# Two products of four feature pairs, run ahead on half of the tokens, as the opening of a SwiGLU FFN

## The chip, the cores and the metric

The kernel runs on one core of a Trainium2 chip. The core has a matrix engine (TensorE, "PE" in the profile, with its weight loads as "PEld"), a vector engine (VectorE, "DVE"), a scalar engine (ScalarE, "ACT"), GpSimd ("POOL") and a queue engine that issues transfers (SyncE, "SP"). Matmuls write to PSUM, which has eight banks here; everything else lies in SBUF, and weights come from HBM by DMA. The metric is device microseconds of one execution; the median of several runs is taken.

## The reference

One layer on 512 tokens of width 1024, all in float32: an FFN, a token mixer (two attention branches, gates and an output projection), and a second FFN of its own weights.

```python
def _swiglu(x, w_gate, w_up, w_down):
    return (jax.nn.silu(x @ w_gate) * (x @ w_up)) @ w_down

f = _swiglu(_rmsnorm(x, ffn1_pre_g[l]), ffn1_w_gate[l], ffn1_w_up[l], ffn1_w_down[l])
x = x + 0.5 * _rmsnorm(f, ffn1_post_g[l])
```

`w_gate` and `w_up` are 1024 x 2816, `w_down` is 2816 x 1024. The change is in how both FFNs compute `x @ w_gate` and `x @ w_up`; the mixer between them is left as it is.

## The kernel before, in words

**Precision.** A float32 factor is split into a high part of reduced mantissa (type fp32r) and the rest, by one copy on ScalarE and one subtraction on VectorE (`split`, L109 to L112). A product then takes three matmuls: high x high, high x low, low x high (`mm3`, L189 to L192).

**Features and pieces.** The 2816 hidden features are 22 groups of 128 (`NF`); here a group is called a feature. For each there is a gate piece and an up piece of the weights, each 128 x 1024 (eight blocks of 128 x 128, one per 128 rows of the model width; 512 KB). The normalised tokens stand transposed in `hn_hi` and `hn_lo`, as model width by tokens, and are the moving operand. Gate and up of one feature are a "pair".

**Ordinary pairs.** `proj_into` (L194) multiplies one piece with the tokens: 8 blocks x 3 matmuls, over 512 tokens or 256. Before the change the first three features (`STD = 3`) are computed so. The first two of them go through `first_pairs` (L217): the last two token tiles are still being normalised and transposed when the FFN begins, so all four pieces are first multiplied with tokens 0 to 255 (24 matmuls of 256 columns each), with the transposes of token tiles 2 and 3 slipped in after two of them (`turns`), and then with tokens 256 to 511. The first piece runs in another order (`proj_first`), all products with the high parts of the tokens first. The third feature goes over the full width of 512 (`pair`, L208).

**Seven products.** The other 19 features are computed with seven block products in place of eight (`seven`, L344). A pair is seen as a 2 x 2 matrix of blocks: the two halves of the model width, by gate and up; the tokens as a 2 x 2 matrix too: halves of the model width by halves of the tokens. Products 1 and 2 are gate times tokens 0 to 255, one for each half of the model width. Products 3 to 7 use sums of weight blocks (named t1 to t4) and sums of token blocks (made once for each FFN by `combined`, L292, from `hn` and from `whole`, unsplit copies of tokens 256 to 511). Each product is 4 blocks x 3 matmuls of 256 columns, 84 for a pair. Products 1, 7, 6 and 4 gather in bank `q`, 5 and 3 in `p`, 2 in `r`; ScalarE and VectorE combine them in `g` and `up`. `use7` applies silu and multiplies.

**Weights.** `load_blocks` (L320) loads one pair's blocks: four transfers on SP's queue, and two on GpSimd's queue that add a second block to one already loaded (L329, L330), so that t1 and t3 arrive as sums. t2 and t4 are added on VectorE (`sums_of`, L335 and L336). `split_block` splits a block into a slot of the pool `w`, which has twelve slots of 128 x 1024. Whole pieces come through `fetch` and `convert` (L122): a load into one of two wide staging buffers (`raw`, L127), then a split of 1024 columns into two slots. A pair by seven products uses one staging buffer too.

**PSUM.** All banks come from one pool of eight (`bank`). A transposed token tile takes two banks (`turned`, L271). For tiles 2 and 3 they are kept until ScalarE has also copied them to `whole` (`kept`, `keep`, L286 to L289): eight copies, run after the last first-half product.

**Order.** From the start of an FFN's head to a mark after the head's first products, the instructions of TensorE, ScalarE and VectorE are pinned to program order among themselves (`ordered`); SP's are until the mixer starts. Elsewhere the framework's scheduler orders each engine's work by its own model, and may also put unpinned work between pinned instructions. Each engine then works strictly in the order it was given.

Of the kernel before, what the change touches and what calls it, by code (L numbers as in the profile page):

```python
# [20 lines left out]
P = 128  # L21
# [13 lines left out]
STD = 3  # L35
# [9 lines left out]
def block_kernel(ctx, tc, x, gains, weights, rpb_near, rpb_all, alibi0, alibi12, out):  # L45
# [71 lines left out]
    state = {"used": False, "next": 0, "take": 0, "stop": 2 * STD, "ahead": lambda: None}  # L117
# [99 lines left out]
    def first_pairs(use, turns, then=None, mid=None):  # L217
# [3 lines left out]
        for i in range(4):  # L221
            (proj_into if i else proj_first)(ps[i], w[i], 0, 256)
            if i in turns:
                late.popleft()()
                if next_norm:
                    next_norm.pop()()
        while kept:
            kept.popleft()()
        if then:
            then()  # L230
        fetch()
        fetch()
        if mid:
            mid(0)
        for i in range(4):
            proj_into(ps[i], w[i], 256, 512)
            if mid and i % 2:
                use(i // 2, *ps[i - 1:i + 1])
                mid(1 + i // 2)
        ordered[-1].append(mark())  # L240
        if not mid:
            use(0, *ps[:2])
            use(1, *ps[2:])


# [45 lines left out]
    def combined():  # L291
# [15 lines left out]
        v = {}  # L307
# [12 lines left out]
    def load_blocks(n):  # L320


        r = wp.tile([P, PIECE], F32, tag="raw", name="raw", bufs=2)
        w11, t1, t3 = unit(name="w11"), unit(name="t1"), unit(name="t3")
        nc.sync.dma_start(t1, weights[n + 1][:, :512])
        nc.sync.dma_start(t3, weights[n + 1][:, :512])
        nc.sync.dma_start(r, weights[n])
        nc.sync.dma_start(w11, weights[n + 1][:, 512:])
        nc.gpsimd.dma_start(t1, weights[n][:, :512], accum_op=ALU.add)  # L329
        nc.gpsimd.dma_start(t3, weights[n + 1][:, 512:], accum_op=ALU.add)  # L330
        return {1: r[:, :512], 2: r[:, 512:], 3: w11, 5: t1, 7: t3}

    def sums_of(raw):
        t2, t4 = unit(name="t2"), unit(name="t4")
        nc.vector.tensor_tensor(t2, raw[5], raw[3], op=ALU.add)  # L335
        nc.vector.tensor_tensor(t4, t2, raw[2], op=ALU.add)  # L336
        raw[6], raw[4] = t2, t4
# [6 lines left out]
    def seven(use, mv, n_pairs, n0, behind, far, lead, raws):  # L344
# [8 lines left out]
        def get(j):  # L353
            if j < n_pairs and j not in raws:
                raws[j] = load_blocks(n0 + 2 * j)
# [3 lines left out]
        def ready(j, i):  # L359
            if j < n_pairs:  # L360
# [4 lines left out]
                blocks[j, i] = split_block(raws[j].pop(i))  # L365
# [18 lines left out]
        for j in range(n_pairs + 1):  # L384
            now, was = j < n_pairs, j > 0
            get(j + 2)
            if now:
                q = product(j, 1, "q", True)
                g, u = res[j] = unit(name="g"), unit(name="up")
                nc.scalar.copy(g[:, :256], q)  # L390
# [10 lines left out]
            if now:  # L401
# [89 lines left out]
    def ffn(g, store, src):  # L491
# [6 lines left out]
        def times(j, a, b):  # L498

            k = feats.index(j)  # L500
            if k >= 2 * m or j < STD:
# [3 lines left out]
            to = lambda i, k: duos[i][k // 2][:, (k % 2) * 256:(k % 2) * 256 + 256]  # L505
            parts = [slice(i * 256, i * 256 + 256) for i in range(2)]
            for i, part in enumerate(parts):
                if duos[i][k // 2] is None:
                    duos[i][k // 2] = unit(name="h")
                nc.vector.tensor_tensor(to(i, k), a[:, part], b[:, part], op=ALU.mult)  # L510
            if k % 2 and hidden[k - 1] is not None:
                for i, part in enumerate(parts):
                    nc.gpsimd.tensor_copy(to(i, k - 1), hidden[k - 1][:, part])
                hidden[k - 1] = None
# [14 lines left out]
        def mid(i):  # L529
            if i == 0:  # L530
                for j in range(2):
# [1063 lines left out]
```

## Time and profile before

| What | Before |
|---|---|
| Timed runs, us | 1087.65, 1087.65, 1088.85 (median 1087.65) |
| Span of the profiled execution, us | 1086.5 |
| TensorE busy | 1076.5 us (99%), 6809 matmuls |
| VectorE / ScalarE / GpSimd busy | 827.5 / 653.1 / 185.6 us |
| Head of the first FFN, from its first product to the first of the seven products | 10.81 to 46.74 us |
| Head of the second FFN | 747.27 to 782.94 us |
| Loaded by SP's queue / by the adding loads of GpSimd's | 131.55 / 52.96 MB |

The profile is of one execution. Its rows name an engine, a line of the kernel (L192), the tiles written and read, shapes, and times in microseconds unless marked ns. In a timeline a row is: start, duration, engine, line, operation, tiles, shapes, count, and in brackets the idle time of the engine before it and what ended it. A timeline joins equal instructions that follow each other into one row. In a table by windows a row is: the window, its length, then for each engine the busy time and the instructions that touch it, the granted clock of TensorE as a share, the busy share of the DMA engines, and GB/s. Matmuls are pipelined, so their recorded durations overlap, and starts are what to compare.

### The profile page before, as it was taken

The page shows a single profiled execution, that of the slowest core. Times are in us where ns is not written, and L with a number is a line of the kernel's source. Part 1 is how long each engine was busy: PE and PEld are TensorE (multiplying, and loading weights), DVE is VectorE, ACT ScalarE, POOL GpSimd, SP SyncE. Part 2 cuts the span into 40 slices and gives each one's busy share as a digit, 9 for nine tenths or more (in the row PEclk, how much of TensorE's full clock was granted, in tenths as well). Part 3 has the DMA queues.
Part 4 walks back from the last instruction along what each step waited for, and adds up shares of the span by engine and source line. Part 5 has one row for each costly group of instructions (what it writes and reads, how often), then busy time and mean ns, then how long its engine had stood idle before and what let it go on. Part 6 is the DMA issues. An engine that isn't in the chain of part 4 may idle for free.

```text
span 1086.5 us, 18606 instructions
## 1 busy us (share of the span) xinstructions
PE 1076.5 (99%) x6809; PEld 975.1 (90%) x6809; DVE 827.5 (76%) x1539; ACT 653.1 (60%) x1315; POOL 185.6 (17%) x252
## 2 busy tenths in 40 slices
PE   9999999999999999999999999999999999999997
PEld 7999999998788988888988888889999999998886
DVE  6887777777988679876467654776897777779985
ACT  6555555564775767767656651375565555565762
POOL 3122111013334000000000001134131111104301
PEclk9999999999999999999999999999999999999999
DMA  6899987569994453422232239664577777759962
GB/s 213 225 210 248 234 219 189 150 169 283 232 264 119 126 182 119 136 83 78 75 102 80 78 107 303 164 111 153 142 187 200 187 176 189 200 181 243 218 198 77
DMA packets 92269, 186.16 MB, mean 171 GB/s; under 512 B 23697, under 2 KB 26257, under 8 KB 92178
## 3 DMA queue, kind: packets, MB, share of 16 engines
q1 hardware_dynamic: 65440, 131.55, 36.2%
q0 software_dynamic: 24048, 52.96, 27.4%
q8 instruction: 53, 0.87, 0.3%
q10 hardware_dynamic: 2690, 0.46, 0.2%
q14 instruction: 38, 0.31, 0.1%
HBM read 179.91 MB, written 7.58 MB: 173 GB/s over the span
## 4 chain that ended last, share of the span: by engine, by line
PE 94%; DVE 3%; DMA 2%; issue 1%; ACT 0%; SPq 0%; POOL 0%; DVEq 0%; POOLq 0%; ACTq 0%
PE ps L190 11%; PE ps L192 11%; PE ps L191 11%; PE q L192 10%; PE q L190 10%; PE q L191 10%; PE p L192 3%; PE p L191 3%; PE p L190 3%; PE r L190 3%; PE r L192 3%; PE r L191 3%; PE c L192 2%; PE c L191 2%; PE c L190 1%; PE ps L991 1%
## 5 line engine op out<-in xcount | busy, mean ns | idle before, releaser
L112 DVE TENSOR_TENSOR w<-raw,w 128x512 fp32r<-128x512 f32 (+1 forms) x136 | 125.7, 926 | 81.3 <-ACT w L111 79.9
L190 PE MATMUL ps<-hn,w 128*128 128x512 f32 (+1 forms) x488 | 174.8, 358 | 0.0
L192 PE MATMUL ps<-hn,w 128*128 128x512 f32 (+1 forms) x488 | 172.4, 353 | 0.0
L191 PE MATMUL ps<-hn,w 128*128 128x512 f32 (+1 forms) x488 | 172.3, 353 | 0.0
L111 ACT CAST w<-raw 128x512 fp32r<-128x512 f32 (+1 forms) x136 | 110.2, 814 | 92.4 <-PE ps L191 49.0
L111 ACT CAST w<-t 128x512 fp32r<-128x512 f32 x152 | 93.7, 619 | 49.0 <-DVE t L335 25.4
L112 DVE TENSOR_TENSOR w<-t,w 128x512 fp32r<-128x512 f32 x152 | 104.1, 689 | 24.4 <-ACT w L111 21.6
L192 PEld LDWEIGHTS ps<-hn,w 128*128 128x128 f32 x488 | 92.3, 189 | 12.8
L191 PEld LDWEIGHTS ps<-hn,w 128*128 128x128 f32 x488 | 92.4, 189 | 11.3
L190 PEld LDWEIGHTS ps<-hn,w 128*128 128x128 f32 x488 | 92.4, 189 | 11.3
L192 PE MATMUL q<-hn,w 128*128 128x256 f32 x304 | 86.0, 283 | 0.0
L190 PE MATMUL p<-v,w 128*128 128x256 f32 x304 | 86.0, 283 | 0.0
L191 PE MATMUL p<-v,w 128*128 128x256 f32 x304 | 86.0, 283 | 0.0
L192 PE MATMUL q<-v,w 128*128 128x256 f32 x304 | 86.0, 283 | 0.0
L190 PE MATMUL q<-v,w 128*128 128x256 f32 x304 | 86.0, 283 | 0.0
L191 PE MATMUL q<-v,w 128*128 128x256 f32 x304 | 86.0, 283 | 0.0
L191 PE MATMUL q<-hn,w 128*128 128x256 f32 x304 | 86.0, 283 | 0.0
L190 PE MATMUL q<-hn,w 128*128 128x256 f32 x304 | 86.0, 283 | 0.0
L192 PE MATMUL p<-v,w 128*128 128x256 f32 x304 | 85.9, 283 | 0.0
L329 POOL DMA_DIRECT2D t<-in_weights_dram x38 | 33.2, 875 | 291.1 <-DMA t<-in_weights_dram 96.6
L190 PE MATMUL q<-w,a 128*128 128x512 f32 x192 | 75.0, 391 | 0.1
L192 PE MATMUL q<-w,a 128*128 128x512 f32 x192 | 74.6, 390 | 0.5 <-DVE a L112 0.5
(262 smaller groups left out, 2998.5 us busy)
## 6 DMA issues: line engine op xcount, KB each, us to landing
raw<-in_weights_dram SPq DMA_DIRECT2D x100, 512.0 KB
t<-in_weights_dram SPq DMA_DIRECT2D x76, 256.0 KB
t<-in_weights_dram POOLq DMA_DIRECT2D x76, 256.0 KB, 5.5
w<-in_weights_dram SPq DMA_DIRECT2D x38, 256.0 KB
rows<-in_weights_dram SPq DMA_DIRECT2D x32, 256.0 KB
w<-in_weights_dram POOLq DMA_DIRECT2D x32, 256.0 KB, 6.8
tb<-in_weights_dram POOLq DMA_DIRECT2D x12, 512.0 KB, 8.2
rows<-in_weights_dram POOLq DMA_DIRECT2D x24, 256.0 KB, 10.3
```

Of the source, the lines that this page charges most:

```text
L111: nc.scalar.copy(hi, src)
L112: nc.vector.tensor_tensor(lo, src, hi.bitcast(F32), op=ALU.subtract)
L190: nc.tensor.matmul(o, sh, mh, start=start, stop=False, **kw)
L191: nc.tensor.matmul(o, sh, ml, start=False, stop=False, **kw)
L192: nc.tensor.matmul(o, sl, mh, start=False, stop=stop, **kw)
L329: nc.gpsimd.dma_start(t1, weights[n][:, :512], accum_op=ALU.add)
L991: nc.tensor.transpose(ps[:, i * P:(i + 1) * P], s, ident)
```

## The change

`STD` goes from 3 to 2, and 20 features instead of 19 are computed by seven products. The head of each FFN no longer multiplies four whole pieces with half of the tokens and then with the other half. Instead it runs products 1 and 2 of the first four features that are computed by seven products (`EARLY = 4`): these need only the gate piece and tokens 0 to 255. Both go into one bank per feature, product 1 in columns 0 to 255 and product 2 in 256 to 511, and their sum is put together in `g` by ScalarE and VectorE at once. The bank stays with the feature as its `q`. Then two ordinary pairs run over all 512 tokens. In `seven`, the first four features leave products 1 and 2 out.

Whole pieces per FFN are eight instead of six: the four gate pieces, and two pieces for each of the two ordinary pairs. The weights are laid out in memory in that order (`_gated_pieces`). For the first four features `load_blocks` reads the second half of the gate piece into the tile of t4 instead of loading the whole gate piece into a staging buffer, and `sums_of` adds to it in place. The sums of tokens (`combined`) are made between the pieces of the two ordinary pairs, and two of the sums a step later than before. The pinned stretch ends after the first of the two ordinary pairs. No feature computed by seven products shares a hidden tile with an ordinary pair any more, so the copies on GpSimd (L513) fall away.

```diff
-STD = 3
+STD = 2
+EARLY = 4
...
-    state = {"used": False, "next": 0, "take": 0, "stop": 2 * STD, "ahead": lambda: None}
+    state = {"used": False, "next": 0, "take": 0, "stop": EARLY + 2 * STD, "ahead": lambda: None}
...
+    def first_products(turns, early):
+
+        w = [take(False) for _ in range(EARLY)]
+        for i in range(EARLY):
+            o = bank("q")
+            for k0 in (0, 4):
+                to = o[:, 64 * k0:64 * k0 + 256]
+                parts = [cut(w[i], k * P, P) for k in range(k0, k0 + 4)]
+                for j in range(4):
+                    for part in parts[j]:
+                        nc.tensor.matmul(to, part, hn_hi[:, k0 + j, 0:256], start=k0 + j == 0 and part is parts[j][0],
+                                         stop=False, skip_group_check=True)
+                for j in range(4):
+                    nc.tensor.matmul(to, parts[j][0], hn_lo[:, k0 + j, 0:256], start=False, stop=j == 3,
+                                     skip_group_check=True)
+            if i in turns:
+                turn_rows()
+            if i == min(turns):
+                fetch()
+            g = unit(name="g")
+            nc.scalar.copy(g[:, :256], o[:, :256])
+            nc.vector.tensor_tensor(g[:, :256], g[:, :256], o[:, 256:], op=ALU.add)
+            early.append((o, g))
+        while kept:
+            kept.popleft()()
+        fetch()
...
-        a = [[unit(name="sum"), unit(name="sum")] for _ in range(2)]
-        for b in range(2):
+        a, v = {}, {}
+
+        def whole_sum(b):
+            a[b] = [unit(name="sum"), unit(name="sum")]
             for i in range(2):
                 nc.vector.tensor_tensor(flat(a[b][i]), view(hn_hi, b, i).bitcast(F32), view(hn_lo, b, i).bitcast(F32), op=add)
-        yield mv
...
+            if n in (6, 3):
+                whole_sum(n == 3)
...
+        nc.sync.dma_start(t1, weights[up][:, :512])
+        nc.sync.dma_start(t3, weights[up][:, :512])
+        raw = {3: w11, 5: t1, 7: t3}
+        if j < EARLY:
+            raw[4] = unit(name="t4")
+            nc.sync.dma_start(raw[4], weights[gate][:, 512:])
+        else:
+            r = wp.tile([P, PIECE], F32, tag="raw", name="raw", bufs=2)
+            nc.sync.dma_start(r, weights[gate])
+            raw[1], raw[2] = r[:, :512], r[:, 512:]
+        nc.sync.dma_start(w11, weights[up][:, 512:])
+        nc.gpsimd.dma_start(t1, weights[gate][:, :512], accum_op=ALU.add)
+        nc.gpsimd.dma_start(t3, weights[up][:, 512:], accum_op=ALU.add)
...
-                blocks[j, i] = split_block(raws[j].pop(i))
+                if j >= EARLY or i not in (1, 2):
+                    blocks[j, i] = split_block(raws[j].pop(i))
...
-                q = product(j, 1, "q", True)
-                g, u = res[j] = unit(name="g"), unit(name="up")
-                nc.scalar.copy(g[:, :256], q)
+                if j < EARLY:
+                    o["q", j], g = early[j]
+                    q = o["q", j][:, :256]
+                else:
+                    q = product(j, 1, "q", True)
+                    g = unit(name="g")
+                    nc.scalar.copy(g[:, :256], q)
...
-            if now:
+            if now and j >= EARLY:
                 r = product(j, 2, "r", True)
...
-        first_pairs(use, (0, 2) if store else (1, 2), mid=mid)
+        early = []
+        first_products((0, 2) if store else (1, 2), early)
+        mv = next(sums)
+        for j in range(2):
+            raws[j] = load_blocks(n0, j)
+        for j in range(STD):
+            ps = [bank(), bank()]
+            for i in range(2):
+                proj_into(ps[i], take(False))
                 next(sums)
+                if j < STD - 1:
+                    fetch()
+            use(j, *ps)
+            if j == 0:
+                ordered[-1].append(mark())
```

More of the change, by code (lines that the diff above doesn't have):

```diff
@@ L215, in pair, with turn_rows, first_pairs @@
         use(j, a, b)
-    def first_pairs(use, turns, then=None, mid=None):
+    def turn_rows():
+        late.popleft()()
+        if next_norm:
+            next_norm.pop()()
+    def first_pairs(use, turns, then):
         w = [take(False) for _ in range(4)]
@@ L223, in first_pairs @@
             if i in turns:
-                late.popleft()()
-                if next_norm:
-                    next_norm.pop()()
+                turn_rows()
         while kept:
             kept.popleft()()
-        if then:
-            then()
+        then()
         fetch()
         fetch()
-        if mid:
-            mid(0)
         for i in range(4):
             proj_into(ps[i], w[i], 256, 512)
-            if mid and i % 2:
-                use(i // 2, *ps[i - 1:i + 1])
-                mid(1 + i // 2)
         ordered[-1].append(mark())
-        if not mid:
-            use(0, *ps[:2])
-            use(1, *ps[2:])
+        use(0, *ps[:2])
+        use(1, *ps[2:])
+    def first_products(turns, early):
[13 more added lines that the diff above has]
+            if i in turns:
+                turn_rows()
+            if i == min(turns):
[7 more added lines that the diff above has]
+        fetch()
     def sumsq(src, acc, f=1.0):
@@ L318, in combined, with load_blocks @@
         yield mv
-    def load_blocks(n):
-        r = wp.tile([P, PIECE], F32, tag="raw", name="raw", bufs=2)
+    def load_blocks(n0, j):
         w11, t1, t3 = unit(name="w11"), unit(name="t1"), unit(name="t3")
[L325 to L331, printed above, removed]
-    def sums_of(raw):
[L334 to L337, printed above, removed]
+        gate, up = (n0 + j, n0 + EARLY + 2 * STD + j) if j < EARLY else [n0 + 2 * STD + 2 * j + i for i in range(2)]
+        nc.sync.dma_start(t1, weights[up][:, :512])
[11 more added lines that the diff above has]
+        nc.gpsimd.dma_start(t3, weights[up][:, 512:], accum_op=ALU.add)
+        return raw
+    def sums_of(raw):
+        raw[6] = unit(name="t2")
+        nc.vector.tensor_tensor(raw[6], raw[5], raw[3], op=ALU.add)
+        if 4 in raw:
+            nc.vector.tensor_tensor(raw[4], raw[6], raw[4], op=ALU.add)
+        else:
+            raw[4] = unit(name="t4")
+            nc.vector.tensor_tensor(raw[4], raw[6], raw[2], op=ALU.add)
     def split_block(raw):
@@ L342, in split_block, with seven @@
         return w
-    def seven(use, mv, n_pairs, n0, behind, far, lead, raws):
+    def seven(use, mv, n_pairs, n0, behind, far, lead, raws, early):
         blocks = {}
@@ L504, in times @@
                 return
-            to = lambda i, k: duos[i][k // 2][:, (k % 2) * 256:(k % 2) * 256 + 256]
-            parts = [slice(i * 256, i * 256 + 256) for i in range(2)]
-            for i, part in enumerate(parts):
+            for i in range(2):
+                part = slice(i * 256, i * 256 + 256)
                 if duos[i][k // 2] is None:
                     duos[i][k // 2] = unit(name="h")
[L510 to L514, printed above, removed]
+                to = duos[i][k // 2][:, (k % 2) * 256:(k % 2) * 256 + 256]
+                nc.vector.tensor_tensor(to, a[:, part], b[:, part], op=ALU.mult)
         def use(j, pg, pu):
@@ L546, in ffn @@
         state["next"] = state["take"] = after + 2 * m + 2
-        seven(use7, next(sums), NF - STD, n0 + 2 * STD, lambda q: [f() for f in q.popleft()], far, lead, raws)
+        seven(use7, mv, NF - STD, n0, lambda q: [f() for f in q.popleft()], far, lead, raws, early)
         rest()
```

26 lines of the change are left out of this document (13 added, 13 removed).

## The prediction

> **What bounds the kernel now.** I read the page first, for the engine that fills the span and for the granted clock.
>
> ```profile
> span 1086.5 us, 18606 instructions
> PE 1076.5 (99%) x6809; PEld 975.1 (90%) x6809; DVE 827.5 (76%) x1539; ACT 653.1 (60%) x1315; POOL 185.6 (17%) x252
> ...
> PEclk9999999999999999999999999999999999999999
> ...
> PE 94%; DVE 3%; DMA 2%; issue 1%; ACT 0%; SPq 0%; POOL 0%; DVEq 0%; POOLq 0%; ACTq 0%
> ```
>
> TensorE is busy for 99% of the span at the full clock, and the chain that ended last runs on it for 94%. So the time is what TensorE issues, plus the few places where it stands still. This execution spans 1086.5 us; the median of the timed runs is 1087.65, so 1.15 us lie around the span, and I add them at the end.
>
> Next come the windows by stage: the two halves of the head of the first FFN (second halves of the first two pairs, then the third pair), the same two of the second FFN, and a stretch in the middle of the seven products.
>
> ```profile
> core 0: us, PE busy (x) PEld busy (x) DVE busy (x) ACT busy (x) POOL busy (x), PEclk, DMA share, GB/s
> 24.32:35.83 11.51, 11.51 (x99) 11.51 (x98) 9.74 (x15) 5.24 (x9) 2.88 (x3) 1.00 0.82 239
> 35.83:46.74 10.91, 10.91 (x51) 9.02 (x50) 8.63 (x14) 6.33 (x11) 2.42 (x3) 1.00 0.70 213
> 760.52:772.03 11.51, 11.51 (x99) 11.51 (x98) 8.53 (x13) 5.15 (x9) 1.08 (x2) 1.00 0.87 217
> 772.03:782.94 10.91, 10.91 (x51) 9.02 (x50) 9.68 (x17) 6.24 (x10) 1.74 (x2) 1.00 0.33 49
> 800.00:840.00 40.00, 40.00 (x336) 40.00 (x335) 31.20 (x58) 23.12 (x49) 6.99 (x8) 1.00 0.76 197
> ```
>
> Each count holds three matmuls still in flight from before the window. So 96 matmuls of 256 columns take 11.51 us, 119.9 ns each; 48 of 512 columns take 10.91 us, 227.3 ns each; and in the seven products 333 matmuls take 40 us, 120.1 ns each. TensorE never stops in these windows. A 512-column matmul costs less than two of 256 (239.8 ns).
>
> **What the change takes from TensorE.** Before, each FFN issues 192 matmuls of 256 columns for pairs 0 and 1 in halves (4 features, 2 halves, 24 each), 48 of 512 for pair 2, and 19 x 84 = 1596 of 256 for the sevens. After, it issues 4 x 2 x 12 = 96 of 256 for the early products, 96 of 512 for two full-width pairs, and 20 x 84 - 96 = 1584 of 256. That is 108 fewer of 256 and 48 more of 512: 108 x 0.120 = 12.96 us less and 10.91 us more, **2.05 us less per FFN, 4.1 us in all**. The early products have the pitch of the first-half products whose place they take, since both issue the same 24 matmuls per piece.
>
> The Trainium skill ("TensorE: Matmul & The Clock Gate", section "Back-to-back issue gap") gives columns / 2.4 + 2.5 ns between isolated matmuls, that is 109.2 and 215.8 ns. The windows here show 120 and 227, with a weight load for each matmul. By the page the gain would be 108 x 0.1092 - 48 x 0.2158 = 1.4 us per FFN, 2.9 in all; the windows are what counts here.
>
> **What it adds on the path: a wait for a PSUM bank.** There are 8 banks. When the fourth early product ends, four hold the early products (their columns are used until their own pair is done), and four hold the transposes of tokens 256 to 511, which are kept until ScalarE has copied them to the whole-token tiles (L289). The first full-width pair needs a new bank at once. Before, the second halves went on in banks they had, and the first new bank was asked for 11.5 us later. In the changed program order on ScalarE, which is pinned here, the copy of the fourth early product stands ahead of those eight copies, and it needs that product's last matmul. These rows of ScalarE, and two of TensorE, price it:
>
> ```profile
> 60.65 0.28 PE L192 MATMUL q<-v,w 128*128 128x256 f32 x1
> 60.77 0.28 PE L190 MATMUL q<-v,w 128*128 128x256 f32 x1
> 60.88 0.28 PE L191 MATMUL q<-v,w 128*128 128x256 f32 x1
> 61.01 0.28 PE L192 MATMUL q<-v,w 128*128 128x256 f32 x1
> ...
> 50.47 0.36 ACT L390 COPY g<-q 128x256 f32<-128x256 f32 x1
> 50.74 0.62 ACT L111 CAST w<-t 128x512 fp32r<-128x512 f32 x1
> ...
> 61.33 0.37 ACT L407 COPY up<-q 128x256 f32<-128x256 f32 x1 [0.71 <-PE q L192]
> ...
> 757.40 1.07 ACT L281 CAST hn<-ps 128x512 fp32r<-128x512 f32 x2 [4.00 <-PE ps L278]
> 758.36 2.33 ACT L289 COPY whole<-ps 128x256 f32<-128x256 f32 x8
> ```
>
> ScalarE began 61.33 - 61.01 = 0.32 us after the start of the last matmul of the product it waited for. The next instruction follows a 256-column copy after 0.27. Two of the eight whole copies (2.33 us together, so 0.27 apart and some 0.4 for the last) are done after 0.67, and the bank is free. With a few hundredths to wake TensorE, 0.32 + 0.27 + 0.67 is 1.3 us from the last matmul's start, against 0.12 without a wait: **1.2 us of standstill per FFN, 2.4 in all** (bounds per FFN: 0 if something covers it, 1.7 if piece 4 comes late, as below). In the row at 758.36 these copies ran during the last first-half product; now ScalarE waits for it, with nothing queued that could go ahead.
>
> **What should stay hidden.** The two pieces of the first full-width pair are now wanted right after the early products. In the first FFN:
>
> ```profile
> 17.60 3.69 SPq L127 DMA_DIRECT2D raw<-in_weights_dram  x2
> 21.35 0.42 SPq L325 DMA_DIRECT2D t<-in_weights_dram  x1
> ...
> 26.71 0.33 SPq L327 DMA_DIRECT2D raw<-in_weights_dram  x1
> ...
> 24.27 2.10 ACT L111 CAST w<-raw 128x1024 fp32r<-128x1024 f32 x2
> 31.40 0.62 ACT L111 CAST w<-raw 128x512 fp32r<-128x512 f32 x1 [5.04 <-DMA raw<-in_weights_dram]
> ...
> 652.55 27.54 SPq L127 DMA_DIRECT2D raw<-in_weights_dram  x5
> ```
>
> Piece 4 is on its way from 17.6 to a nearly empty queue. A load of the same size from 26.71, in a full one, landed by 31.40, 4.7 us later; so piece 4 lands by 22.3 at the latest. Its split (1.05 us on ScalarE, 1.22 on VectorE, row below) is ordered behind the first two transposes; queued behind it on ScalarE are the copies of the second and third early product and of the last transposes (1.07), which the full-width pair reads from 24.3 on. With a landing at 21 all of that is done by 23.5; at 22.3 it runs to 24.9 and adds 0.5 to the wait for the bank. I take the earlier one, since the queue is empty. The second piece has 5.45 us more (24 x 0.227). In the second FFN both pieces are loaded well ahead: the last row above is SP's last issue of whole pieces before that head, and it ends at 680.
>
> Four small copies, four adds, six DMA issues of a pair turning into four plus two, and the dropped GpSimd copies cost nothing on the path as long as VectorE keeps up. Its durations:
>
> ```profile
> L112 DVE TENSOR_TENSOR w<-t,w 128x512 fp32r<-128x512 f32 x12 | 8.0, 684 | 0.0
> ...
> L112 DVE TENSOR_TENSOR w<-raw,w 128x1024 fp32r<-128x1024 f32 x2 | 2.4, 1222 | 2.3 <-ACT w L111 2.3
> ...
> L503 DVE TENSOR_TENSOR h<-ps,h 128x512 f32<-128x512 f32 x3 | 2.1, 686 | 1.0 <-ACT h L518 1.0
> ...
> L403 DVE TENSOR_TENSOR g<-g,r 128x256 f32<-128x256 f32 x2 | 0.8, 415 | 0.0
> ```
>
> Between the early products and the sevens it gets two more whole pieces (2 x 1.22) and up to four adds (4 x 0.42), and loses one product of a pair (0.69) and the low parts of two blocks prepared ahead (2 x 0.68): about 2.1 us more. Its idle time there is 22.42 - 18.37 = 4.05 us in the first FFN and 22.42 - 18.21 = 4.21 in the second, by the four windows. So it fits, with 2 us over. In the sevens VectorE has 31.20 / 40 x 10.08 = 7.9 us per pair; an early pair loses two low parts and an add (1.8) and so needs 6.1 of TensorE's 60 x 0.12 = 7.2. Loads: an early pair moves 1.5 MB instead of 1.75, in 7.2 us instead of 10.08, some 20% faster, against a DMA share of 0.76; it no longer needs one of the two wide staging buffers, so its loads may start earlier.
>
> The sum: 1086.5 - 4.1 + 2.4 = 1084.8 for the span, plus 1.15: **1086.0 us** (rounded up), 0.15% less than before, which is within the 0.2% below which a measurement of this kernel can't be told from no change. The range of this case alone is 1085.2 to 1086.8 (a wait of 0.8 to 1.6 per FFN).
>
> **Rivals.**
>
> *A, the bank wait is covered.* The whole 4.1 us stay: 1083.6. For it: the chain is TensorE's, nothing else is late. Against it: eight banks, eight holders, and the order on ScalarE is fixed.
>
> *B, VectorE's stretch before the sevens is full, and the change is slower.* VectorE works in order. In the second FFN it stood idle before these:
>
> ```profile
> 770.17 0.69 DVE L112 TENSOR_TENSOR w<-raw,w 128x512 fp32r<-128x512 f32 x1 [1.76 <-ACT w L111]
> 770.78 0.68 DVE L112 TENSOR_TENSOR w<-t,w 128x512 fp32r<-128x512 f32 x1
> 771.38 0.68 DVE L112 TENSOR_TENSOR w<-raw,w 128x512 fp32r<-128x512 f32 x1
> ...
> 773.65 0.69 DVE L503 TENSOR_TENSOR h<-ps,h 128x512 f32<-128x512 f32 x1 [0.98 <-ACT h L518]
> ...
> 782.61 0.69 DVE L335 TENSOR_TENSOR t<-t,w 128x512 f32<-128x512 f32 x1
> ```
>
> Three blocks were ready ahead, 4.3 us of products, and the sums of the first pair came only at 782.61, when TensorE was about to begin the sevens at 782.94. If the idle time is of that kind (waits in order) and can't be filled, the added 2.1 us go straight through, and with fewer blocks ready ahead TensorE waits some 2.2 us at the first seven-pair of each FFN: 1086.0 + 4.4 = 1090.4. It decides from 0.9 us per FFN on (no gain is left) and is slower by 0.2% from 2.0. Against it: the 4 us are twice what is added.
>
> *C, the third early load is late in the first FFN.* Pieces 6 and 7 now stand on SP's queue behind eight block loads.
>
> ```profile
> q1 hardware_dynamic: 65440, 131.55, 36.2%
> q0 software_dynamic: 24048, 52.96, 27.4%
> ...
> 25.69 1.07 POOL L329 DMA_DIRECT2D t<-in_weights_dram  x1 [7.39 <-DMA t<-in_weights_dram]
> 26.49 1.20 POOL L330 DMA_DIRECT2D t<-in_weights_dram  x1
> 34.77 0.87 POOL L329 DMA_DIRECT2D t<-in_weights_dram  x1 [7.07 <-DMA t<-in_weights_dram]
> ```
>
> The plain queue moves 131.55 MB / (0.362 x 1086.5 us) = 334 GB/s alone, the adding one 178. From 21.3, piece 5, eight blocks of 262 KB and piece 6 are 3.15 MB, 9.4 us; each adding load of 262 KB in between takes 1.5. With two of them piece 6 lands at 33.7, with four at 36.6. It is wanted at 25.4 + 10.9 = 36.3 less 2.3 for the split: 34.0. I take two, as the adds of the second pair came at 34.77 before. With four it is late by 2.6; half of that gives 1087.3.
>
> **How the numbers follow.** Forecast 0.45, A 0.14, B 0.24, C 0.17. A third of the forecast's 0.45 I put under 1085.5 (0.2% below), the rest is no change; A is faster; of C 0.15 is no change and 0.02 slower; of B 0.04 is no change. So faster 0.15 + 0.14 = 0.29, same 0.30 + 0.15 + 0.04 = 0.49, slower 0.22. The range goes from A to just short of B's time, 1083.5 to 1090.2; what lies beyond is about half of B.
>
> **What would show it.** A pitch of 0.227 us over two full pairs in both FFNs and 60 matmuls per early pair shows the saving; TensorE standing still about 1.2 us in front of the first full-width matmul, released by the whole copies, shows the bank. A wait at the first product with a combined moving block, released by VectorE, would show B; a wait of a full-width pair on the split of piece 6, ended by a DMA, C. No gap at the bank, or one over 1.7 us, would make the sum wrong.

## The result and the profile after

The changed kernel takes 1097.73 us (median of five runs, 1095.61 to 1099.1) against 1087.65 us for the kernel before on the same chip: 1.0082 times as long, 95% interval 1.0071 to 1.0093. The forecast was 1086.0 us, the range ended at 1090.2.

The profiled execution is the second fastest of the five, 1096.21 us, with a span of 1094.4 us, 7.9 us more than before. First the page, then windows over the first full-width pair and around the place where TensorE stands longest (columns as in the prediction's windows):

```profile
span 1094.4 us, 18389 instructions
...
PE 1077.8 (98%) x6689; PEld 971.0 (89%) x6689; DVE 834.7 (76%) x1553; ACT 655.8 (60%) x1325; POOL 181.4 (17%) x252
...
PE 90%; DVE 4%; DMA 2%; ACT 2%; issue 1%; POOL 0%; SPq 0%; DVEq 0%; POOLq 0%; ACTq 0%
```

```profile
26.44:37.35 10.91, 10.91 (x48) 9.04 (x49) 8.35 (x14) 6.56 (x14) 3.64 (x4) 1.00 1.03 307
...
790.00:795.20 5.20, 0.74 (x7) 0.53 (x5) 2.01 (x5) 0.85 (x3) 1.34 (x2) 1.00 1.07 267
795.20:800.00 4.80, 4.71 (x26) 4.71 (x27) 3.77 (x8) 3.29 (x8) 2.13 (x3) 0.64 1.10 262
```

The saving came: there are 120 matmuls fewer, 60 per FFN, and a full-width pair runs at the old pitch, 10.91 us for 48 matmuls. What was lost stands in the waits of TensorE's weight loads (total, times, longest):

```profile
PEld p L191 <- ACT up L441: 4.8, 1, 4.8
PEld ps L191 <- ACT whole L312: 3.9, 2, 2.4
...
PEld ps L193 <- DVE w L113: 1.7, 4, 0.5
```

From the distances between matmul starts (a start that comes later than the pitch), the 7.9 us are:

| Place | us |
|---|---|
| 120 matmuls fewer (108 of 256 columns less and 48 of 512 more, per FFN) | -4.1 |
| Bank wait ahead of the first full-width pair, FFN 1 (24.83) and FFN 2 (760.72) | +1.5, +2.4 |
| Full-width pairs waiting for the low halves of pieces 6 and 7, both FFNs (1.1 without the late start of the matmul behind each wait, 1.5 with it) | +1.3 |
| First pairs of the sevens in FFN 2 (790.46) | +4.7 |
| Half clock behind that wait: 4.80 us at 0.64 granted | +1.7 |
| First product later (11.62 against 10.81) | +0.8 |
| Waits elsewhere (before 0.67 at 274.37 and 0.24 at 1056.09, after 0.52 at 1063.93) | -0.4 |

They add up to 7.9, with some 0.2 us of play. The 0.8 us is the run's, not the change's: in the kernels below, whose beginning is the same, the first product starts anywhere from 10.6 to 12.3. Between the medians lie 10.1 us: the other four timed runs had a lower mean granted clock (0.993 to 0.996) than the profiled one (0.998), so they may hold more half clock than the 1.7 us here, but no trace of them is kept.

Who held the bank, and what came late at the sevens? ScalarE, in the second FFN's head, and then at the long wait:

```profile
757.73 0.59 ACT L304 CAST hn<-ps 128x512 fp32r<-128x512 f32 x1 [2.50 <-PE ps L301]
758.33 1.28 ACT L560 ACT_TABLE_LOAD   x1
759.63 0.73 ACT L560 ACTIVATE g<-g 128x256 f32<-128x256 f32 x2
760.26 0.57 ACT L304 CAST hn<-ps 128x512 fp32r<-128x512 f32 x1
760.72 0.38 ACT L262 COPY g<-q 128x256 f32<-128x256 f32 x1
761.91 0.42 ACT L560 ACTIVATE g<-g 128x256 f32<-128x256 f32 x1 [0.81 <-DVE g L263]
762.23 0.35 ACT L262 COPY g<-q 128x256 f32<-128x256 f32 x1
762.49 1.75 ACT L312 COPY whole<-ps 128x256 f32<-128x256 f32 x6
...
794.35 0.62 ACT L112 CAST w<-t 128x512 fp32r<-128x512 f32 x1 [5.54 <-DMA t<-in_weights_dram]
794.87 0.37 ACT L441 COPY up<-p 128x256 f32<-128x256 f32 x1
```

L560 is the silu of an early product, with the load of its table. In the program it comes only in `use7`, much later; its input is ready here, and the scheduler put it in the pinned stretch, between the copies. At 794.35 the split of a block stands ahead of the copy that frees `p`, and that split waits 5.54 us for a transfer. SP's queue in that head, first before the change, then after (a long row of SP is one in which it waited):

```profile
751.98 1.63 SPq L325 DMA_DIRECT2D t<-in_weights_dram  x1
...
755.60 0.38 SPq L328 DMA_DIRECT2D w<-in_weights_dram  x1
762.91 1.46 SPq L327 DMA_DIRECT2D raw<-in_weights_dram  x2
```

```profile
757.06 10.29 SPq L128 DMA_DIRECT2D raw<-in_weights_dram  x2
767.40 0.42 SPq L350 DMA_DIRECT2D t<-in_weights_dram  x1
...
774.87 6.46 SPq L358 DMA_DIRECT2D raw<-in_weights_dram  x2
781.43 0.37 SPq L350 DMA_DIRECT2D t<-in_weights_dram  x1
```

Both long rows are loads into a wide staging buffer (two exist) that is still in use: at 757.06 pieces 6 and 7, at 774.87 the gate pieces of pairs 4 and 5. SP's waits for them, 9.5 us and 9.2 us in all, are ended by splits of pieces on VectorE, which set a buffer free. The blocks of early pairs 2 and 3 are issued from 781.43 on, behind them. SP's order in this FFN is the scheduler's. In the first FFN SP is pinned to program order; there the same blocks are issued at 31.7 and 47.35, and no such wait occurs.

### The profile page after: what moved, and what is told of

The parts are those of the page before. It is cut to its first block, busy times and chain, and to the rows that moved or that the text cites. A ratio compares the mean times of both kernels' runs of the same rounds, so it can differ in the third digit from the quotient of the medians.

```text
span 1094.4 us, 18389 instructions
## 1 busy us (share of the span) xinstructions
PE 1077.8 (98%) x6689; PEld 971.0 (89%) x6689; DVE 834.7 (76%) x1553; ACT 655.8 (60%) x1325; POOL 181.4 (17%) x252
## 4 chain that ended last, share of the span: by engine, by line
PE 90%; DVE 4%; DMA 2%; ACT 2%; issue 1%; POOL 0%; SPq 0%; DVEq 0%; POOLq 0%; ACTq 0%
PE q L191 10%; PE q L193 10%; PE q L192 10%; PE ps L191 9%; PE ps L193 9%; PE ps L192 9%; PE p L191 3%; PE p L193 3%; PE p L192 3%; PE r L193 2%; PE r L192 2%; PE r L191 2%; PE c L192 2%; PE c L193 2%; PE c L191 2%; DVE w L113 1%
## 5 line engine op out<-in xcount | busy, mean ns | idle before, releaser
L113 DVE TENSOR_TENSOR w<-raw,w 128x1024 fp32r<-128x1024 f32 (+1 forms) x128 | 122.5, 957 | 76.2 <-ACT w L112 76.0
L112 ACT CAST w<-raw 128x1024 fp32r<-128x1024 f32 (+1 forms) x128 | 107.3, 839 | 88.6 <-PE ps L192 41.5
L191 PE MATMUL ps<-hn,w 128*128 128x512 f32 (+1 forms) x408 | 155.5, 381 | 3.5 <-ACT whole L312 3.5
L193 PE MATMUL ps<-hn,w 128*128 128x512 f32 (+1 forms) x408 | 153.6, 376 | 0.4 <-DVE w L113 0.2
L192 PE MATMUL ps<-hn,w 128*128 128x512 f32 (+1 forms) x408 | 153.1, 375 | 0.0
L112 ACT CAST w<-t 128x512 fp32r<-128x512 f32 x160 | 97.2, 619 | 54.5 <-DVE t L367 29.0
L113 DVE TENSOR_TENSOR w<-t,w 128x512 fp32r<-128x512 f32 x160 | 108.9, 689 | 25.8 <-ACT w L112 23.4
L191 PE MATMUL p<-v,w 128*128 128x256 f32 x320 | 90.9, 285 | 4.6 <-ACT up L441 4.6
L191 PEld LDWEIGHTS ps<-hn,w 128*128 128x128 f32 x408 | 76.9, 188 | 16.4 <-ACT whole L312 3.9
L192 PE MATMUL p<-v,w 128*128 128x256 f32 x320 | 90.9, 284 | 0.0
L191 PE MATMUL q<-v,w 128*128 128x256 f32 x320 | 90.8, 284 | 0.0
L193 PE MATMUL p<-v,w 128*128 128x256 f32 x320 | 90.8, 284 | 0.0
L192 PE MATMUL q<-v,w 128*128 128x256 f32 x320 | 90.8, 284 | 0.0
L193 PEld LDWEIGHTS ps<-hn,w 128*128 128x128 f32 x408 | 76.8, 188 | 15.6 <-DVE w L113 1.7
L193 PE MATMUL q<-v,w 128*128 128x256 f32 x320 | 90.6, 284 | 0.0
L192 PEld LDWEIGHTS ps<-hn,w 128*128 128x128 f32 x408 | 77.0, 189 | 12.5
L193 PE MATMUL q<-hn,w 128*128 128x256 f32 x288 | 81.5, 283 | 0.0
L191 PE MATMUL q<-hn,w 128*128 128x256 f32 x288 | 81.5, 283 | 0.0
L192 PE MATMUL q<-hn,w 128*128 128x256 f32 x288 | 81.5, 283 | 0.0
```

The lines of the kernel that those rows point to most:

```text
L112: nc.scalar.copy(hi, src)
L113: nc.vector.tensor_tensor(lo, src, hi.bitcast(F32), op=ALU.subtract)
L191: nc.tensor.matmul(o, sh, mh, start=start, stop=False, **kw)
L192: nc.tensor.matmul(o, sh, ml, start=False, stop=False, **kw)
L193: nc.tensor.matmul(o, sl, mh, start=False, stop=stop, **kw)
```

## The experiments

Two theories. Theory 1: the lost time is order on in-order engines, and none of it is capacity. Theory 2: the DMA engines cannot bring the blocks of early pairs, which now pass in 7.2 us each. Beside them stands the prediction's rival B, VectorE full before the sevens. Each comparison shares one set of runs of the kernel before (medians 1087.65 to 1088.51), so ratios are what to compare.

For the traces, this table gives how much earlier (-) or later (+) than in the changed kernel one and the same matmul starts, in us: the 401st (first FFN, in its third early pair), the 2001st (behind the first FFN), the 4572nd (second FFN, in its first full-width pair) and the 4742nd (behind the long wait and the half clock). The first product itself starts at 11.62 in the changed kernel; it starts 0.7 earlier in keep, sp and all, 0.5 and 0.3 earlier in best and calm, at the same time in spfar, 0.3 later in mix and low, and 0.7 later in silu, and that is in the figures.

| Kernel | 401st | 2001st | 4572nd | 4742nd |
|---|---|---|---|---|
| keep | -0.5 | -0.3 | -1.8 | -1.7 |
| sp | -0.3 | -0.3 | -0.3 | +0.3 |
| silu | +0.9 | +0.9 | -0.3 | +1.3 |
| all | +2.4 | +2.9 | +0.6 | -5.5 |
| spfar | -0.3 | -0.3 | -0.3 | -6.6 |
| mix | -0.1 | +1.7 | -0.8 | -2.1 |
| low | +0.7 | +0.7 | +2.3 | -2.4 |
| best | -0.8 | +0.7 | -1.8 | -8.9 |
| calm | -1.3 | -1.3 | -3.8 | -10.9 |

### keep: the whole copies ahead of the fourth early product's copy

```diff
@@ first_products
+            if i == EARLY - 1:
+                while kept:
+                    kept.popleft()()
             g = unit(name="g")
             nc.scalar.copy(g[:, :256], o[:, :256])
...
-        while kept:
-            kept.popleft()()
         fetch()
```

> Edit: in both FFN heads the eight whole copies run ahead of the copy of the fourth early product on ScalarE, not behind it. Theory 1 (order on in-order engines): the waits for a PSUM bank in front of the first full-width matmul (1.5 us in the first FFN, 2.4 in the second) fall to under 0.3 in the first and to about 1.2 in the second, where a table load and three silus stand in the same stretch; the 4.7 us wait at the sevens of the second FFN stays. In all 2 to 3 us less than the changed kernel. Theory 2 (loads: the early pairs take their blocks faster than DMA brings them, wherever the wait stands): TensorE only arrives earlier at the same late load; the wait at the sevens grows by as much, and the time stays within 0.5 us of the changed kernel.

Measured: 1096.11 us, ratio 1.0081 (1.0059 to 1.0103). The ratio is that of the changed kernel (1.0082), so the 2 to 3 us of theory 1 did not come. The bank waits fell to 1.19 and 0.87 us (theory 1 had under 0.3 in the first FFN), and part of that came back at once: the wait for the low half of piece 6 grew from 0.22 to 0.70 us in both FFNs, since VectorE reaches that split no earlier. By the 4572nd matmul this execution is 1.8 us ahead, 0.7 of them from its earlier first product, and it meets a shorter but still long wait at the sevens (4.2 us).

### sp: SP in program order from the early products to the end of the full-width pairs

```diff
@@ ffn
+        sp_from = mark()
         first_products((0, 2) if store else (1, 2), early)
...
             if j == 0:
                 ordered[-1].append(mark())
+        pool.append((sp_from, mark(), (mybir.EngineType.SP,)))
```

> Edit: in the head of the second FFN SP's queue is held to program order, so that the block loads of the first two seven-pairs are issued ahead of whole pieces 6 and 7 and do not queue behind their wait for a staging buffer. Theory 1: the block loads start near 752 instead of 767, the wait of 4.7 us at the sevens of the second FFN is gone, the clock is not lowered behind it, and the time falls by 5 to 7 us against the changed kernel, to about 1091. Theory 2 (DMA can't bring the early pairs' blocks in their 7.2 us): at least 3 us of the wait stay, somewhere in the first four pairs, and the time falls by less than 3 us.

Measured: 1096.16 us, ratio 1.0074 (1.0059 to 1.0089). SP's queue of this kernel:

```profile
752.01 0.45 SPq L350 DMA_DIRECT2D t<-in_weights_dram  x1
...
756.75 10.29 SPq L128 DMA_DIRECT2D raw<-in_weights_dram  x2
774.56 6.46 SPq L358 DMA_DIRECT2D raw<-in_weights_dram  x2
781.13 0.37 SPq L350 DMA_DIRECT2D t<-in_weights_dram  x1
```

The blocks of pairs 0 and 1 now go first, at 752, as before the change; the long wait stays (4.84 us). Theory 1 had 1091: it named the wrong entry of the queue: not the load that waits at 757, but the next, at 774.56, decides. Between 770 and 780 the DMA share is 0.19: the engines are nearly idle while loads stand behind a waiting one, which speaks against theory 2.

### silu: the silu of a first half behind that of its second half

```diff
@@ use7
-            nc.scalar.activation(g[:, :256], g[:, :256], AF.Silu)
-            nc.scalar.activation(g[:, 256:], q, AF.Silu)
+            b = nc.scalar.activation(g[:, 256:], q, AF.Silu)
+            with tc.issue_after(b.ins if hasattr(b, "ins") else b):
+                nc.scalar.activation(g[:, :256], g[:, :256], AF.Silu)
```

> Edit: the silu of the first half of a seven-pair is issued behind that of its second half, so that ScalarE can't take it (and its table load) in the head of an FFN. Theory 1: the wait for a bank falls from 2.4 to about 1.2 us in the second FFN and from 1.5 to about 1.2 in the first, 1.5 us in all; the 4.7 us at the sevens stay. Theory 2: TensorE arrives earlier at the same late load, and the time stays as it is within 0.5 us.

Measured: 1095.87 us, ratio 1.0071 (1.0053 to 1.009). Without the silu in between the bank waits are 1.17 us in both FFNs, the prediction's 1.2. So 1.2 was the price of the program's order, and the silu with its table load makes it 2.4 in the second FFN. In the first FFN the silu is not the whole of it: with it in place the wait is 1.69 in sp, where the split of piece 4 begins 11.2 us behind the first product, and 1.17 in spfar, where it begins 10.3 behind it. The time does not follow (the ratio is 0.0011 lower, inside the interval): a wait of 0.84 us comes at the first seven-pair of the second FFN, the long wait (4.6 us) stands behind it, and the half clock lasts 6.8 us in place of 3.4.

### all: the three orders, and pieces 6 and 7 split ahead of the sums of tokens

```diff
@@ ffn, beside the edits of keep, sp and silu
                 proj_into(ps[i], take(False))
-                next(sums)
                 if j < STD - 1:
                     fetch()
+                next(sums)
```

> Edit: the three together (whole copies first, SP in program order in the second head, silu kept out of the head), and each whole piece is split ahead of the token sums that stand before it, not behind. Theory 1: no wait over 0.5 us is left in either head; the 4.1 us of matmul time come through, and the time is 1083 to 1086, less than the kernel before. Theory 2: waits of 3 us and more stay at the first seven-pairs of both FFNs, and the time is over 1089.

Measured: 1091.02 us, ratio 1.0027 (1.0015 to 1.0039). That misses the 1083 to 1086 of theory 1. The long wait in the second FFN is gone (under 0.5 us at a time), though SP's order is that of sp, in which it stayed: with pieces 6 and 7 split sooner the staging buffers come free sooner, and the blocks of pairs 2 and 3 are issued from 776.79 in place of 781.13. The first FFN got a new one. TensorE's waits, and ScalarE there:

```profile
PE q L191 <- ACT w L112: 1.8, 1, 1.8
...
PE p L191 <- ACT up L442: 1.0, 2, 0.8
```

```profile
34.17 1.05 ACT L112 CAST w<-raw 128x1024 fp32r<-128x1024 f32 x1 [3.23 <-DMA raw<-in_weights_dram]
...
49.78 0.62 ACT L112 CAST w<-t 128x512 fp32r<-128x512 f32 x1 [1.29 <-DVE t L368]
```

Piece 6 lands at about 34.1, where the prediction's C had it (33.7 with two adding loads). With its split ahead of the sums of tokens everything behind it on VectorE is late by that: VectorE stands 3.6 us until 35.25, and the sums of the first pair's blocks come only at 49. That is B's price (a wait of 2 us at the first seven-pair), brought about by C's late landing. The order of the changed kernel, sums first, was right for the first FFN.

### spfar: SP in program order until the ordinary seven-pairs of the second FFN

```diff
@@ ffn, in place of the edit of sp
         seven(use7, mv, NF - STD, n0, lambda q: [f() for f in q.popleft()], far, lead, raws, early)
+        if store:
+            pool.append((sp_from, state['sevens'], (mybir.EngineType.SP,)))
@@ seven
             get(j + 2)
+            if j == EARLY:
+                state['sevens'] = mark()
```

> The changed kernel, with SP's loads of the second FFN pinned to program order from the early products until the first ordinary seven-pairs are under way: the blocks of early pairs 2 and 3 then stand ahead of the two gate pieces of pairs 4 and 5, which wait for a wide staging buffer. Theory 1 (order on in-order queues): SP was the cause of the 4.7 us wait at the first seven-pairs and of the half clock behind it (1.7 to 3.4 us); the blocks of pairs 2 and 3 are issued by about 770 instead of 781, the wait is under 1 us, the clock stays full, and the time is 1089 to 1092. The waits at the bank (1.5 and 2.4) and on the low halves of pieces 6 and 7 (0.7 per FFN) stay. Theory 2 (the DMA engines can't bring the blocks of the early pairs in 7.2 us each): the loads are issued early but land late all the same, the wait stays above 3 us, and the time stays above 1094.

Measured: 1091.12 us, ratio 1.0025 (1.0014 to 1.0035), inside the range of theory 1. SP's queue, then two windows of this kernel, and one of sp:

```profile
767.61 0.37 SPq L350 DMA_DIRECT2D t<-in_weights_dram  x1
...
778.14 0.44 SPq L358 DMA_DIRECT2D raw<-in_weights_dram  x1
```

```profile
770.00:780.00 10.00, 9.90 (x44) 7.84 (x44) 9.56 (x15) 5.79 (x10) 3.47 (x4) 1.00 1.04 306
...
790.00:800.00 10.00, 10.00 (x86) 10.00 (x85) 8.58 (x17) 4.00 (x9) 1.73 (x2) 1.00 0.88 185
```

```profile
770.00:780.00 10.00, 9.94 (x44) 7.89 (x44) 9.57 (x15) 5.79 (x10) 0.00 (x0) 1.00 0.19 53
```

Pair 2's blocks are issued at 767.6 in place of 781.4, the loads run in a stretch where the DMA engines were nearly idle in sp (0.19 from 770 to 780, 1.04 here), and TensorE runs through 790 to 800 at the full clock. By the 4742nd matmul this one edit is worth 6.3 us (-0.3 at the 4572nd, -6.6 behind). The DMA engines do bring the blocks in time: theory 2 falls for the second FFN.

### mix: three orders, SP left alone

The edits of keep and silu, and, for the full-width pairs, the products with the low part of the weight last:

```diff
+    def proj_low_last(o, w):
+        for k in range(NK):
+            for m in (hn_hi, hn_lo):
+                nc.tensor.matmul(o, cut(w, k * P, P)[0], m[:, k, 0:T], start=k == 0 and m is hn_hi, stop=False)
+        for k in range(NK):
+            nc.tensor.matmul(o, cut(w, k * P, P)[1], hn_hi[:, k, 0:T], start=False, stop=k == NK - 1)
@@ ffn
-                proj_into(ps[i], take(False))
+                proj_low_last(ps[i], take(False))
```

> The changed kernel with three orders changed and SP left alone: the whole copies stand ahead of the copy of the fourth early product; the silu of a first half stands behind that of its second half, so that none gets between the copies; and in the two full-width pairs the products with the low part of the weight stand last in each feature (16 matmuls, 3.6 us, later than before). Theory 1: the bank waits fall to about 0.6 in the first FFN and under 0.3 in the second, the waits on the low halves of pieces 6 and 7 (0.7 per FFN) go to 0, the 4.7 us wait and the half clock stay: 1097.7 - 0.9 - 2.1 - 1.4 = 1093.3, range 1092 to 1094.5. If the waits only move along (VectorE as the limit, rival B of the prediction), new waits of 1 us or more appear at the first seven-pair of the first FFN, and the time stays at 1095 or above.

Measured: 1093.36 us, ratio 1.0045 (1.0031 to 1.0058). The forecast was met, but not in the way it said, so by luck: the bank waits are gone altogether (in the first FFN the first product also began late and stood 0.45 us), while 0.67 us came at piece 6 (now its high half), 0.64 at the first seven-pair and 1.52 at 90.9 in the first FFN, and the long wait went to 3.7.

### low: the low parts last, alone

The edit shown under mix, nothing else.

> The changed kernel with one order changed: in the two full-width pairs the products with the low part of the weight stand last in each feature. Theory 1: only the waits of the full-width pairs on the low halves of pieces 6 and 7 go (0.33 + 0.44 us in the first FFN, the same in the second: 1.1 to 1.5 in all, some 1096 against 1097.7); bank waits of 1.5 and 2.4 and the 4.7 us at the sevens stay. If VectorE is full before the sevens (rival B), the waits come back at the first seven-pair of each FFN, 0.5 to 1 us each, and the time stays at 1097 to 1098.

Measured: 1093.27 us, ratio 1.0048 (1.0034 to 1.0062), 3 us better than theory 1 had it. The waits for the low halves went; in the first FFN they came back as 0.92 us at the first seven-pair. A split on ScalarE ends that wait; ScalarE works without a pause from 47.94, when the first block sum on VectorE lets it begin, so this is rival B's way at one remove. The rest came from elsewhere, by the 4742nd matmul:

```profile
789.37 0.36 ACT L448 COPY up<-p 128x256 f32<-128x256 f32 x1
795.00 0.62 ACT L112 CAST w<-t 128x512 fp32r<-128x512 f32 x1 [5.27 <-DMA t<-in_weights_dram]
```

```profile
763.85:768.00 4.15, 4.15 (x11) 3.30 (x12) 1.58 (x2) 2.85 (x8) 0.00 (x0) 0.59 0.00 0
```

The late block lands as in the changed kernel (795.0 against 794.35), but here the copy that frees `p` stands ahead of its split, not behind it, so TensorE had one product more (12 matmuls, 1.4 us) done when it had to wait. And the clock fell behind the bank wait at 763.85 (4.15 us at 0.59, 1.7 us lost), where the coming wait hid it. So the run does not price the low halves; it shows that in the part that the scheduler orders an edit at one place changes the order at another.

### best: the three orders of mix and SP's order of spfar

> The three orders of the run before and SP's order together. Theory 1 (all the lost time is order, none of it is capacity): the saving of 4.1 us stays but for 0.6 to 1 us at the bank, 1087.65 - 4.1 + 0.8 = 1084.4, range 1083.6 to 1086. Theory 2 (DMA rate): a wait of 3 to 5 us at the first seven-pairs of the second FFN stays, 1088 to 1092. Rival B (VectorE's stretch before the sevens is full): waits of 1 to 2 us at the first seven-pair of each FFN, 1086.5 to 1089.

Measured: 1085.77 us (1084.67 to 1086.64), ratio 0.9974 (0.9963 to 0.9985): faster than the kernel before. Its waits on TensorE that the changed kernel's head has to do with:

```profile
PE q L191 <- ACT g L440: 1.3, 1, 1.3
...
PE ps L203 <- ACT whole L320: 0.9, 1, 0.9
PE p L193 <- DVE w L113: 0.5, 1, 0.5
```

All three are in the first FFN (at 90.17, 24.53 and 51.04; 1.42, 1.01 and 0.63 us by the starts); in the second no wait over 0.15 us is left in the head. So the order is nearly all of the loss: theory 1 holds, at the upper end of its range.

### calm: best, with the bias loads behind the early pairs

In the first FFN the loads for the mixer's bias tables go out on SP one by one between the blocks of the seven-pairs.

```diff
@@ ready
-                if j and loads:
+                if j > EARLY and loads:
                     loads.popleft()()
```

> The kernel with all four orders changed (the three on ScalarE and TensorE, and SP's), with one more edit: the loads of the bias tables, which the first FFN issues on SP one by one between the blocks of the seven-pairs, begin behind the four early pairs instead of with the second one. In the kernel without this edit TensorE still stood 0.63 us at 51.0 and 1.42 us at 90.2 in the first FFN, the second one for a block that came late. If the bias loads crowd SP's queue and the DMA engines where the early pairs need a block set every 7.2 us, the wait at 90 goes (1.4 us less), that at 51 perhaps too: 1085.77 - 1.4 = 1084.4, range 1083.7 to 1085. If it is the rate of the blocks themselves or VectorE, both waits stay and the time is 1085.5 to 1086.3.

Measured: 1085.11 us (1084.33 to 1085.84), ratio 0.9971 (0.9961 to 0.9982). The wait at 90 is gone, that at 51 stays:

```profile
span 1083.4 us, 18403 instructions
```

```profile
PE ps L203 <- ACT whole L320: 0.6, 1, 0.6
PE p L193 <- DVE w L113: 0.5, 1, 0.5
```

The forecast of 1084.4 (to 1085) is just missed. In best the wait at 90 stood behind a product into `r`, which only ordinary seven-pairs have, so the late block was not an early pair's: loads were tight in the first FFN behind the early pairs, where the bias loads share queue and engines with them. That the early pairs themselves can't be fed in 7.2 us, which was theory 2, no run shows. From the 1086.5 us before, 4.1 saved, and 0.7 at the bank, 0.6 at the sevens, 0.5 at the start and 0.5 less elsewhere give 1083.7; the span is 1083.4. Against `best` the gain in the medians (0.7 us, from two sets of runs) is not certain; the wait's end is seen in the trace.

### vec: calm, with the first pair's block sums on GpSimd

```diff
-    def sums_of(raw):
+    def sums_of(raw, eng=None):
+        eng = eng or nc.vector
         raw[6] = unit(name="t2")
-        nc.vector.tensor_tensor(raw[6], raw[5], raw[3], op=ALU.add)
+        eng.tensor_tensor(raw[6], raw[5], raw[3], op=ALU.add)
...
-                    sums_of(raws[j])
+                    sums_of(raws[j], None if j else nc.gpsimd)
```

> The kernel with the four orders changed and the bias loads moved back, with the two block sums of early pair 0 in each FFN (two adds of 128x512, 0.65 us each on VectorE) computed on GpSimd, which idles there from 31 to 44 us. If VectorE's full stretch before the sevens (rival B, in its small remainder) causes the wait left at 50.6 us in the first FFN (0.63 us, on the low part of a block), 1.3 us less on VectorE ends it, and the time is 1085.1 - 0.6 = 1084.5 (range 1083.8 to 1085). If the wait is set by the blocks' loads or by ScalarE, it stays at 0.5 us or more and the time at 1085.1.

Measured: 1087.06 us, ratio 0.9988 (0.9979 to 0.9997), slower than calm where 0.6 us less was forecast. The wait at 51 is gone (0.06 us), but mostly because TensorE comes there later: it starts the same matmul at 51.16, against 51.30 in calm, having reached it 0.43 us later. That the wait was VectorE's is seen in calm: a split on VectorE ends it, and VectorE works without a pause from 43.34 to 53.5. TensorE now stands 1.00 us at 41.19 and 0.86 at 770.27, both for the high half of piece 7. GpSimd and VectorE of this kernel, then VectorE of calm at the same work:

```profile
33.53 1.45 POOL L376 TENSOR_TENSOR t<-t,w 128x512 f32<-128x512 f32 x1 [2.30 <-DVE sum L326]
35.06 1.61 POOL L378 TENSOR_TENSOR t<-t,t 128x512 f32<-128x512 f32 x1
...
33.92 3.30 DVE L113 TENSOR_TENSOR v<-sum,v 128x512 fp32r<-128x512 f32 x2
```

```profile
34.52 1.30 DVE L113 TENSOR_TENSOR v<-sum,v 128x512 fp32r<-128x512 f32 x2
```

While GpSimd adds, two splits take VectorE 3.30 us in place of 1.30. VectorE lost 2.0 us to be spared 1.3, and the sums behind it, which stand ahead of piece 7's split on ScalarE, are late.

## Why the prediction was wrong, step by step

**The saving: right.** 120 matmuls fewer at pitches of 0.120 and 0.227 us.

**The bank wait: right mechanism, mis-sized term.** Forecast 1.2 us per FFN, measured 1.5 and 2.4. The step that failed is that the order on ScalarE "is pinned here": pinned instructions keep their order among themselves, but others may be put between them, as the text on the kernel's order said, and the early products had just made the silu of their first halves ready. With the silu out of the way (silu) it was 1.17 in both. In the first FFN piece 4 also landed late: its split waited for the transfer until 22.39, near the prediction's upper bound of 22.3 and not at the 21 that I chose "since the queue is empty".

**"So it fits, with 2 us over": half right.** Summed over the stretch VectorE's idle time did take the added work: in the changed kernel no wait of a seven-pair on VectorE over 0.15 us is seen in the first FFN. But the sum said nothing on order within the stretch: the low halves of pieces 6 and 7 stand behind sums of tokens, and the full-width pairs waited 1.3 us for them. Once TensorE came earlier (low, best, calm), 0.6 to 0.9 us of rival B appeared at the first seven-pair of the first FFN (ended by VectorE in best and calm, by ScalarE behind it in low). B's mechanism was real, its price a third of the 2.2 us.

**"six DMA issues of a pair turning into four plus two ... cost nothing on the path", "its loads may start earlier": the step that failed.** The sum puts this term at nothing. It costs 4.7 us and then 1.7 at half clock, 6.4 of the 12.0 us between what the saving alone would give and what was measured in the span. I weighed how much the loads move and how fast, not what stands ahead of them. Eight whole pieces in place of six and then pairs 4 and 5 ask for the two staging buffers, and on SP's one queue whatever waits for a buffer holds up the early pairs' blocks, which need neither. I worked out the order on SP's queue for pieces 6 and 7 (rival C), in the first FFN, where SP is pinned and where it turned out harmless as long as the sums go first; for the second FFN, whose order is the scheduler's, I left it out. Spfar shows the step: SP's order alone takes the 6.3 us back.

**The rivals.** A, the whole saving: in no run. In best and calm 0.7 to 1.0 us at the bank stay in the first FFN, where piece 4 lands late; in mix, whose first product began 0.6 to 0.7 us later than theirs, the bank cost nothing, and other waits took its place. B and C: present, small, and above all tied to each other (all). The actual cause was none of the three, which is why the range missed it. The forecast's number comes out when the orders are mended: 1085.77 and 1085.11 us. That it is so near is in part luck: the bank wait is 0.7 to 1.0 us in one FFN in place of 1.2 in two, since the whole copies were moved ahead, and other waits (0.6 at the first seven-pair, 1.4 at 90 in best) stand in its place.

## What to carry to other kernels

A change that starts work earlier also makes new instructions ready early and asks for buffers early; list for each in-order engine, the DMA queues above all, what the scheduler may put ahead of the work that is wanted next, and look at every place where that order is not written out by hand. Here a transfer that waited for a buffer held up all that stood behind it on its queue, with the DMA engines at 0.19 in sp. Idle time summed over a stretch says that work fits, not that it is done when it is wanted; and a wait that is removed ahead of a larger one may gain little, so mend the last one first (spfar alone took the ratio from 1.0082 to 1.0025, keep and silu alone to 1.0081 and 1.0071, inside their intervals).

## What the runs showed of the hardware

**The clock after a standstill.** The length of a wait does not say what the granted clock does behind it: behind 2.36 us at the bank it stayed full in the changed kernel, and behind the same wait at the same place it fell in low. In the traces every fall and rise of the clock behind the first product lies a whole number of 3.413 us from the moment at which it first became full (230 and 231 of them in the changed kernel, 10.60 to 795.67 and 799.08). Cut into such windows, the waits do tell:

| Kernel | Window, us | TensorE stands still in it, us (by the matmul starts) | Granted clock of the next window |
|---|---|---|---|
| changed, at the bank | 758.12 to 761.54 | 0.70 | 1.00 |
| changed, at the bank | 761.54 to 764.95 | 1.65 | 1.00 |
| low, at the bank | 760.68 to 764.09 | 2.37 | 0.50 |
| low, at the sevens | 791.40 to 794.81 | 1.45 | 1.00 |
| sp, at the sevens | 789.40 to 792.82 | 2.54 | 0.50 |
| all, first FFN, two waits | 48.65 to 52.06 | 2.77 | 0.50 |
| changed, at the sevens | 788.84 to 792.26 | 1.68 | 1.00 |
| changed, at the sevens | 792.26 to 795.67 | 3.03 | 0.50 |

Keep (2.74), silu and mix (3.41 each) agree. So up to 1.68 us of standstill in a window left the clock full, and from 2.37 us on the whole next window ran at half, which costs up to 1.7 us (in sp and silu two windows in a row did); where the limit lies between them no run shows. The Trainium skill ("TensorE: Matmul & The Clock Gate", Part 1, "What's actually happening") has a window of 3413 ns that runs freely, and a low clock after an idle window. The traces agree with the length and with the free run, which is why equal waits differ; that 2.37 us of standstill in a window can already do it, the section does not lead one to expect.

**GpSimd beside VectorE.** Two adds of 128x512 on GpSimd stretched two subtractions of the same size on VectorE from 1.30 to 3.30 us (vec). The Trainium skill ("SBUF — State Buffer", section "Who interferes with whom") says that a VectorE instruction with two inputs in SBUF contends with a GpSimd instruction that reads SBUF, and that the lock between them is exclusive. The run agrees: 2.0 us lost beside 3.1 us of GpSimd.
